# Expert weights of an encoder block: loads of two neighbouring channels per partition, in six places of 22,528 bytes

## Chip, core and metric

The kernel runs on one core of a Trainium2 chip. The metric is the device time of one execution in microseconds (us), as the median of three runs. The core has five engines that run their own instruction streams: TensorE (PE, with PEld for its weight loads), VectorE (DVE), ScalarE (ACT), GpSimd (POOL) and SyncE (SP). SP issues every load here; the bytes are moved by the core's 16 DMA engines.

## What is computed

One layer of an encoder for 512 tokens of 1,024 channels, in float32: a mixing layer (windowed attention beside a gated MLP, then an output projection), and then 16 experts, each of which picks its 64 best tokens. Cut to what matters here:

```python
mod = jax.nn.silu(c) @ w_ada[l] + b_ada[l]
shift1, scale1, gate1, shift2, scale2, gate2 = jnp.split(mod, 6, axis=-1)
h = modulate(rms_norm(x, norm_pre_mix[l]), shift1, scale1)
proj = h @ w_in[l]
...                                              # attention and gated MLP -> mix
x = x + gate1[:, None, :] * rms_norm(mix @ w_out[l], norm_post_mix[l])
h2 = modulate(rms_norm(x, norm_pre_ffn[l]), shift2, scale2)
aff = softmax(h2 @ w_router); gates, idx = top_k(aff^T, 64)          # per expert
xs = h2[idx]
hid = silu(xs @ w_gate[e]) * (xs @ w_up[e])      # w_gate, w_up: 16 x 1024 x 2816
out = (hid @ w_down[e]) * gates                  # w_down: 16 x 2816 x 1024
x = x + gate2[:, None, :] * rms_norm(scatter_add(out, idx), norm_post_ffn[l])
```

The weights of the experts are 16 x 3 x 11.53 MB = 553.6 MB of the 593.6 MB that the kernel reads. Each is used once.

## The kernel before

**Stages.** The kernel is one straight program without loops on the chip. First comes the mixing layer (x transposed, modulations from `w_ada`, input projection, attention, gated MLP, output projection), then the experts, one after the other. Within the mixing layer the steps of attention and projection are interleaved by a hand-written table (`at_step`); a scheduler of the framework then fixes each engine's order, and an engine runs its instructions strictly in that order.

**The weights' loads.** The helper `chunk` (lines 831 to 836) allocates a tile, has SP load it, and returns it. A load of before is 128 partitions of 2,816 float32: 11,264 contiguous bytes for each partition, 1.44 MB in all. `up_proj` takes one load for each of the eight row tiles of 128 channels of `w_gate` or `w_up` (partition p holds channel p of the tile); `expert` takes eight loads for `w_down`. So an expert has 24 loads, and the 16 experts have 384 such pieces.

**Places.** The 13 places of these loads come from four pools, in the order `ORDER`: six in `sl`, whose places serve all loads of the mixing layer too (weights of the input projection, `w_ada`, `w_out`) and which stays open from the first line to the last; three in `s2p`, which hold parts of `w_out` for the gated MLP's half of the output projection (`wz`) until then; three in `s3p` on the right side, over what attention had (`at`, closed behind the last attention step); one in `s4p`, over what the output projection had (`ow`). For the first expert two more loads go to three tiles of the mixing layer (`in_places`). A new tile waits for those that had its bytes before.

**Lanes.** Each DMA takes the next of eight completion semaphores (named DMAHW0 to DMAHW7), and waits for the DMA that had it before. So at most eight are under way.

**An expert.** `route` ranks the tokens and gathers the chosen rows with matmuls (`px`), transposes them and applies scale and shift (`pxt`); `hidden` does the gate and the up projection, multiplies, and transposes the result (`pht`); `expert` does the down projection (`pd`) and adds the rows back with matmuls (`pys`). `last_expert` takes the down projection in three parts of the channels with smaller loads (two DMAs each, runs of 2,048 or 1,024 bytes), so that what follows the last bytes is short.

Of the kernel before, what the change touches and what calls it, by code (L numbers as in the profile page):

```python
# [7 lines left out]
F32 = mybir.dt.float32  # L8
# [21 lines left out]
N1, N2, N3, N4 = 6, 3, 3, 1  # L30
# [5 lines left out]
ORDER = (0,) * N1 + (1,) * N2 + (2,) * N3 + (3,) * N4  # L36
XK = len(ORDER) - KD
# [14 lines left out]
def encoder_block(ctx, tc, x, c, w_ada, b_ada, norm_pre_mix, norm_post_mix, w_in, sink, sgu_ln_g,  # L52
# [33 lines left out]
    prm = ea.tile([P, 2, P], F32, name="prm")  # L86
    col, prows = {}, {}
# [15 lines left out]
    # columns of w_ada for shift1, scale1 of 128 channels with the rows of w_in for q, k, v of these channels  # L103
# [18 lines left out]
    def more_loads():  # L122
        nonlocal wsT, lng, lnb, wst, nsink, wr
        n1 = params(1, (("npf", by_row(norm_pre_ffn[0]), 8), ("pom", by_row(norm_post_mix[0]), 8),
# [9 lines left out]
        nc.sync.dma_start(wr, w_router[0].rearrange("(k p) e -> p k e", p=P))  # L134
# [9 lines left out]
    # ---------------------------------------------------------------- constants  # L144
# [24 lines left out]
    def make_dist():  # L169
        """|distance|, or a huge number outside the window; keys in front of, of, behind the block"""  # L170
# [10 lines left out]
    def rsqrt(dst, v, n):  # L181
        """dst = 1/sqrt(v) for [P, n] f32, to f32's accuracy: a guess from the bits, then Newton."""
# [19 lines left out]
    def rms(src, n, junk, dst=None):  # L202
        """1/rms of the rows of src (one [P, n] or two halves of it)"""
# [12 lines left out]
    # ---------------------------------------------------------------- parameters by column  # L216
    pc = [cp.tile([P, 64], F32, name=f"pc{i}") for i in range(2)]
# [16 lines left out]
    for o in (8, 32):  # L234
        nc.vector.tensor_scalar(pcol("ba", o, 8), pcol("ba", o, 8), 1.0, None, op0=OP.add)

    # ---------------------------------------------------------------- x: transposed; 1 / rms
# [29 lines left out]
    # ---------------------------------------------------------------- shift1, scale1; h  # L267
# [7 lines left out]
    def mod_rows(pm, col, w, n, first, last):  # L275
        """w [P, 4, n]: four column tiles of the array add col^T w at once"""
        for j in range(4):
            nc.tensor.matmul(pm[32 * j:32 * j + 32, :n], col.to_broadcast([P, 32]), w[:, j],
                             start=first, stop=last, tile_position=(0, 32 * j))

    def mod_cols(rows, n):
        """the four rows of rows [P, n] as columns: [P, n / 128, 4] in PSUM"""
# [5 lines left out]
    def mod1_rows(k):  # L288
        """PE: even and odd rows of w_ada in column tiles of their own"""
# [19 lines left out]
    def mod1_acc(k):  # L309
        """DVE: the sums over a partition's rows"""  # L310
# [25 lines left out]
    # ---------------------------------------------------------------- input projection  # L336
# [3 lines left out]
    def split(hi, lo, src):  # L340
        """src as a sum of two parts that float32r holds"""
# [10 lines left out]
    def qkv(k):  # L352
        """heads j and j + 4 of q share a block of rows; then k, v"""
# [43 lines left out]
    param_cols(1, prows[1])  # L397
    nc.vector.tensor_scalar(nsink, nsink, -1.0, None, op0=OP.mult)
# [43 lines left out]
    def attn_out(n, j):  # L442
        """the same heads' outputs, transposed"""
# [32 lines left out]
    def attn_end(n, j0, j1):  # L476
        """heads j0 .. j1 and those 4 on, in two parts, and their squares"""
# [17 lines left out]
    # ---------------------------------------------------------------- gMLP  # L495
# [13 lines left out]
    def spatial():  # L509
        """u (W_s vn + b_s), in place of u"""  # L510
# [25 lines left out]
    # ---------------------------------------------------------------- the other modulations  # L536
# [7 lines left out]
    def mod2(i, kk):  # L544
        """gate1, shift2, scale2, gate2: two row tiles of their columns at a time, summed over a partition's rows"""
# [11 lines left out]
    def mod2_cols(i):  # L557
        pm = bank("pm2")
        mod_rows(pm, ones, acc[i].rearrange("p (j w) -> p j w", j=4), 256, True, True)
# [3 lines left out]
        nc.vector.tensor_tensor(mods[:, i].rearrange("p (j q) -> p q j", j=4), m,  # L563
# [4 lines left out]
        elif i == 2:  # L568
            nc.vector.tensor_tensor(s2, s2, pcol("npf", 0, 8), op=OP.mult)
# [9 lines left out]
    def spread(dst, cols):  # L579
        """dst [P, D]: every row the vector whose columns are given"""  # L580
# [8 lines left out]
    # ---------------------------------------------------------------- the mixing layer, interleaved  # L589
# [495 lines left out]
```

## Time and profile before

| | before |
|---|---|
| median of 3 runs | 1546.35 us (1544.28 to 1550.43) |
| span of the profiled execution | 1544.5 us |
| PE busy / DVE / ACT / POOL | 1387.1 / 429.7 / 188.9 / 116.0 us |
| moved by DMA | 596.86 MB, 386 GB/s over the span |
| loads of 1.44 MB | 128 gate, 126 up, 120 down (and two up loads in parts, 18 + 6 smaller down loads) |

The profiled execution's span, 1544.5 us from its first to its last instruction, lies within the times of the three runs and 1.85 us under their median. It has two regimes. Up to about 270 us the mixing layer runs, with the engines busy and the DMA engines partly idle. From there to about 1,522 us the experts' weights stream in without a pause that a slice of the profile would show. Then a tail of some 22 us finishes the last expert and writes the output. [...]

### The profile page before, as it was taken

To read this page: it belongs to the slowest core of one execution; us is meant where nothing else is said; L and a number is where in the kernel's file an instruction comes from. 1 tells how busy PE (TensorE), PEld (TensorE's weight loads), DVE (VectorE), ACT (ScalarE), POOL (GpSimd) and SP (SyncE) were. 2 spreads that over 40 slices of the span, in tenths; PEclk is the share of its full clock that TensorE was granted. 3 is DMA by queue.
4 is the path that set the end of the run, shared out by engine and by line. 5 is a ranking of instruction groups with operands and counts; after the bars stand their busy time and mean duration, and the time that the engine had idled before them with its cause. 6 is when DMAs were issued, how large, how long until landed. Compare 5 with 4: busy or idle time off the path is not lost.

```text
span 1544.5 us, 17570 instructions
## 1 busy us (share of the span) xinstructions
PE 1387.1 (90%) x7282; PEld 619.8 (40%) x7282; DVE 429.7 (28%) x1087; ACT 188.9 (12%) x404; POOL 116.0 (8%) x144
## 2 busy tenths in 40 slices
PE   7888998999999998998898998989898989898986
PEld 5665665343444433333333333324242423333323
DVE  5789857112112120212112111112020303020104
ACT  3336433000010000000100000000000000000001
POOL 2457310000000000000000000000000000000002
PEclk9998999999999999999999999999999999999998
DMA  9776608999999999999999999999999999999995
GB/s 316 275 252 181 241 6 334 415 411 428 429 429 429 429 429 428 429 428 429 429 428 429 429 429 429 429 428 429 429 428 429 429 429 429 428 429 429 429 396 202
DMA packets 92711, 596.86 MB, mean 386 GB/s; under 512 B 8692, under 2 KB 31960, under 8 KB 44760
## 3 DMA queue, kind: packets, MB, share of 16 engines
q1 hardware_dynamic: 92632, 595.74, 93.3%
q8 instruction: 57, 0.93, 0.2%
q14 instruction: 22, 0.18, 0.0%
HBM read 593.62 MB, written 2.10 MB: 386 GB/s over the span
## 4 chain that ended last, share of the span: by engine, by line
DMA 60%; PE 28%; DVE 8%; issue 1%; ACT 1%; POOL 1%; SPq 0%; DVEq 0%; ACTq 0%; POOLq 0%
DMA w<-in_w_down_dram 23%; DMA w<-in_w_up_dram 19%; DMA w<-in_w_gate_dram 18%; PE pf L949 11%; PE pd L991 4%; PE px L888 1%; PE pys L1001 1%; PE py L348 1%; PE py L346 1%; PE po L462 1%; PE py L347 1%; DVE ex L851 1%; PE pd L1031 1%; DVE racc L555 1%; DVE acc L317 1%
## 5 line engine op out<-in xcount | busy, mean ns | idle before, releaser
L949 PE MATMUL pf<-w,ex 128*64 128x512 f32 (+1 forms) x3072 | 638.0, 561 | 42.0 <-DMA w<-in_w_up_dram 40.6
L949 PEld LDWEIGHTS pf<-w,ex 128*64 128x64 f32 x3072 | 215.0, 137 | 433.2 <-issue 326.2
L991 PE MATMUL pd<-w,ex 128*64 128x512 f32 (+1 forms) x1440 | 319.3, 563 | 33.7 <-DMA w<-in_w_down_dram 33.7
L991 PEld LDWEIGHTS pd<-w,ex 128*64 128x64 f32 x1440 | 109.9, 136 | 231.7 <-issue 126.0
L967 DVE TENSOR_TENSOR ex<-pf,ex 128x512 f32<-128x512 f32 (+1 forms) x48 | 30.4, 647 | 362.3 <-PE pf L949 362.0
L995 DVE TENSOR_SCALAR ex<-pd,gc 128x512 f32<-128x512 f32 x15 | 11.3, 751 | 377.6 <-PE pd L991 377.6
L907 POOL COPY ex<-ex 128x512 f32<-128x512 f32 x16 | 9.8, 613 | 1138.2 <-DVE ex L905 1058.0
L888 PE MATMUL px<-x_sb,ex 128*64 128x256 f32 x512 | 71.0, 386 | 8.6 <-DVE ex L864 7.4
L919 ACT ACTIVATE ex<-pot 128x512 f32<-128x512 f32 x16 | 9.6, 597 | 544.6 <-PE pot L917 544.6
L1007 DVE TENSOR_TENSOR y<-pys,y 128x512 f32<-128x512 f32 x112 | 68.2, 681 | 17.0 <-PE pys L1001 17.0
L974 ACT ACTIVATE ex<-pht 128x512 f32<-128x512 f32 (+1 forms) x48 | 23.5, 559 | 374.6 <-PE pht L973 374.6
L1001 PE MATMUL pys<-ex 64*128 64x512 f32 x240 | 55.6, 602 | 12.7 <-DVE ex L995 12.7
L900 DVE TENSOR_SCALAR ex<-pxt,mods 128x64 f32<-128x64 f32 x128 | 34.9, 337 | 92.0 <-PE pxt L895 92.0
L888 PEld LDWEIGHTS px<-x_sb,ex 128*64 128x64 f32 x512 | 41.3, 136 | 38.3 <-DVE ex L864 18.8
L851 DVE SCALAR_TENSOR_TENSOR ex<-rt,afs,before 128x512 f32<-128x512 f32 (+2 forms) x65 | 46.8, 719 | 12.3 <-PE rt L858 12.3
L913 DVE COPY gc<-pgc 128x1 f32<-128x1 f32 x16 | 2.5, 158 | 152.6 <-PE pgc L910 152.6
L555 DVE SCALAR_TENSOR_TENSOR racc<-ada,cs,racc 128x1024 f32<-128x1024 f32 x28 | 42.6, 1521 | 0.2
L959 ACT ACTIVATE ex<-pf 128x512 f32<-128x512 f32 (+1 forms) x48 | 26.9, 561 | 121.2 <-PE pf L949 120.4
L1001 PEld LDWEIGHTS pys<-ex 64*128 64x128 f32 x240 | 21.9, 186 | 47.1 <-DVE ex L995 25.9
L973 PE MATMUL pht<-ident,ex 128*128 128x128 f32 x176 | 25.7, 295 | 12.1 <-DVE ex L967 12.1
L973 PEld LDWEIGHTS pht<-ident,ex 128*128 128x128 f32 x176 | 22.7, 213 | 22.7 <-DVE ex L967 22.7
L890 ACT ACTIVATE ex<-px 128x256 f32<-128x256 f32 x32 | 12.3, 383 | 125.7 <-PE px L888 125.6
(254 smaller groups left out, 1086.3 us busy)
## 6 DMA issues: line engine op xcount, KB each, us to landing
w<-in_w_gate_dram SPq DMA_DIRECT2D x128, 1408.0 KB, 26.8
w<-in_w_up_dram SPq DMA_DIRECT2D x126, 1408.0 KB, 26.8
w<-in_w_down_dram SPq DMA_DIRECT2D x120, 1408.0 KB, 26.8
ada<-in_w_ada_dram SPq DMA_DIRECT2D x16, 1024.0 KB, 6.5
w<-in_w_down_dram SPq DMA_DIRECT2D x18, 512.0 KB, 9.6
wq<-in_w_ada_dram SPq DMA_DIRECT2D x16, 512.0 KB, 5.9
wi<-in_w_in_dram SPq DMA_DIRECT2D x4, 1024.0 KB, 5.2
wq<-in_w_in_dram SPq DMA_DIRECT2D x8, 384.0 KB, 6.2
```

Source lines behind the costliest of these rows:

```text
L555: nc.vector.scalar_tensor_tensor(acc[i], t[:, r], cs[:, k:k + 1], acc[i], op0=OP.mult, op1=OP.add)
L851: nc.vector.scalar_tensor_tensor(junk[:, :c1 - c0], p[:, c0:c1], afs[:, b, e:e + 1], before[:, o + c0:o + c1], op0=OP.subtract, op1=OP.is_ ...
L888: nc.tensor.matmul(px[i][h * CAP:(h + 1) * CAP, :256], ohr[:, b], x_sb[:, b, c0:c0 + 256], start=(b == 0), stop=(b == NB - 1))
L900: nc.vector.tensor_scalar(xs[:, k], pt[:, c0:c0 + CAP], s2[:, k:k + 1], sh2[:, k:k + 1], op0=OP.mult, op1=OP.add)
L949: nc.tensor.matmul(pb[n][h * 64:(h + 1) * 64, :NW[n]], XS[e][:, k], t, start=(i == 0), stop=(i == KD - 1))
L959: nc.scalar.activation(hid[:, n * 512:n * 512 + NW[n]], pg[n][:, :NW[n]], AF.Silu)
L967: nc.vector.tensor_tensor(hs, pu[n][:, :NW[n]], hs, op=OP.mult)
L973: nc.tensor.transpose(p[:, j * P:(j + 1) * P], hv[:, j0 + j], ident)
L974: nc.scalar.activation(hT[:, j0:j0 + n], p.rearrange("p (j t) -> p j t", j=4)[:, :n], AF.Copy)
L991: nc.tensor.matmul(pd[dh * 64:(dh + 1) * 64, c0:c0 + n], hT[:, j, h * CAP:(h + 1) * CAP], t[:, o - q * FF:o - q * FF + n], start=(h == 0 a ...
L1001: nc.tensor.matmul(p, OT[e][dh * 64:(dh + 1) * 64, b * P:(b + 1) * P], oe[dh * 64:(dh + 1) * 64, :], start=True, stop=True)
L1007: nc.vector.tensor_tensor(yb, p, yb, op=OP.add)
```

## The change

A load now takes two neighbouring channels per partition: partition p of a load of `w_gate` or `w_up` holds channels 2p and 2p + 1 of 256 channels, 22,528 contiguous bytes, 2.88 MB in all; for `w_down` a load is twice as wide as before. An expert has 12 loads. The four pools become two: `wl` with five places on the left side, `wrt` with one on the right. So that they can lie there, `sl` and `s2p` become phases that are closed behind the mixing layer, with `outw`. The first expert's third load of `w_up` goes to the three tiles of the mixing layer, in three DMAs.

Since a partition now has neighbouring channels, all that meets these weights by channel is laid out in pairs: the rows of `w_router`, shift2, scale2 and norm_pre_ffn (`pair_cols`, `prm2`, `pp`), the transposes for the router and for the chosen rows (a step of two in the free axis), and two modulations' columns. The matmuls of an expert's gate and up projections are the same in number and size; those of the down projection are 44 of 512 columns in place of 40 of 512 and 8 of 256.

```diff
-N1, N2, N3, N4 = 6, 3, 3, 1
+N1, N2 = 6, 3
+NL, NR = 5, 1
...
-ORDER = (0,) * N1 + (1,) * N2 + (2,) * N3 + (3,) * N4
-XK = len(ORDER) - KD
+ORDER = (0,) * 3 + (1,) * NR + (0,) * (NL - 3)
+XK = 2 * (len(ORDER) - KD // 2)
...
-    sl = ctx.enter_context(tc.tile_pool(name="sl", bufs=N1))
...
+    closeS, sl = phase("sl", "left", N1)
     closeE, ea = phase("early", "left")
...
+        nc.sync.dma_start(wr.rearrange("p (m i) e -> p m (i e)", i=2),
+                          w_router[0].rearrange("(m p i) e -> p m (i e)", p=P, i=2))
+        nc.sync.dma_start(prm2[:8], b_ada[0, 3 * D:5 * D].rearrange("(r w) -> r w", w=2 * P))
+        nc.sync.dma_start(prm2[8:], norm_pre_ffn[0].rearrange("(r w) -> r w", w=2 * P))
...
+    def pair_cols():
+        p = bank("pp")
+        for i in range(2):
+            nc.tensor.transpose(p[:, i * 12:(i + 1) * 12], prm2[:, i::2], ident[:12, :12])
+        nc.vector.tensor_copy(pp, p[:, :24].rearrange("p (i r) -> p i r", i=2))
+        nc.vector.tensor_scalar(pp[:, :, 4:8], pp[:, :, 4:8], 1.0, None, op0=OP.add)
...
-                nc.tensor.transpose(p[:, k * P:(k + 1) * P], xb[:, (i * 4 + k) * P:(i * 4 + k + 1) * P], ident)
+                c0 = (2 * i + k // 2) * 2 * P
+                nc.tensor.transpose(p[:, k * P:(k + 1) * P], xb[:, c0 + k % 2:c0 + 2 * P:2], ident)
...
-        s2p = ctx.enter_context(tc.tile_pool(name="s2p", bufs=N2, side="left", reuse_waits="tile"))
+        closeW, s2p = phase("s2p", "left", N2)
         closeO, ow = phase("outw", "left")
...
-    closeO.close()
-    s4p = ctx.enter_context(tc.tile_pool(name="s4p", bufs=N4, side="left", reuse_waits="tile"))
-    s3p = ctx.enter_context(tc.tile_pool(name="s3p", bufs=N3, side="right", reuse_waits="tile"))
+    for c in (closeO, closeW, closeS):
+        c.close()
+    wl = ctx.enter_context(tc.tile_pool(name="wl", bufs=NL, side="left", reuse_waits="tile"))
+    wrt = ctx.enter_context(tc.tile_pool(name="wrt", bufs=NR, side="right", reuse_waits="tile"))
...
-    def chunk(ap, shape=(FF,)):
+    def chunk(ap, shape=(2 * FF,)):
...
-        t = (sl, s2p, s3p, s4p)[ORDER[i]].tile([P] + list(shape), F32, name="w", tag="slot")
+        t = (wl, wrt)[ORDER[i]].tile([P] + list(shape), F32, name="w", tag="slot")
...
-        for i, k in enumerate(KORD):
-            rows = [w[0, e, kk * P:(kk + 1) * P, :] for kk in KORD[i:i + 2]]
...
+        for j, m in enumerate(MORD):
+            rows = w[0, e, m * 2 * P:(m + 1) * 2 * P, :].rearrange("(p i) f -> p (i f)", i=2)
+            parts = in_places(rows) if j == extra else [(chunk(rows), 0, 2 * FF)]
+            for i in range(2):
...
-            for q in range(4):
-                t = chunk(wd[:, q * FF:(q + 1) * FF])
...
+            for q in range(2):
+                t = chunk(wd[:, 2 * q * FF:2 * (q + 1) * FF])
```

The order of SP's instructions changes. Before, behind the last two loads of `w_ada` for the mixing layer (`ada`), stand the first loads of `w_gate`, up to those that wait for TensorE; names in brackets are the semaphores that a row waits for: DMAHW0 to DMAHW7 the lanes of earlier DMAs, the others the engines.

```order
L547 DMA ada_1781<-in_w_ada_dram 128x2x1024 [waits DMAHW3_49,DVE_49,Activation_49]
L547 DMA ada_1785<-in_w_ada_dram 128x2x1024 [waits DMAHW4_49,DVE_49,Activation_49]
L835 DMA w<-in_w_gate_dram 128x2816 [waits DMAHW6_49,DMAHW5_49,DVE_49]
L835 DMA w<-in_w_gate_dram 128x2816 [waits DMAHW0_49,DMAHW7_49,DVE_49,Activation_49]
L835 DMA w<-in_w_gate_dram 128x2816 [waits DMAHW1_49,DVE_49]
L835 DMA w<-in_w_gate_dram 128x2816 [waits DMAHW2_49,DVE_49]
L835 DMA w<-in_w_gate_dram 128x2816 [waits DMAHW3_49,DVE_49]
L835 DMA w<-in_w_gate_dram 128x2816 [waits DMAHW4_49,DVE_49]
L835 DMA w<-in_w_gate_dram 128x2816 [waits PE_49] x2
L835 DMA w<-in_w_up_dram 128x2816 [waits DMAHW5_49,PE_49]
L835 DMA w<-in_w_up_dram 128x2816 [waits DVE_49,DMAHW6_49,PE_49,Activation_49]
L835 DMA w<-in_w_up_dram 128x2816 [waits DMAHW7_49,Pool_49]
```

Of the changed kernel, the same place on SP:

```order
L564 DMA ada_1788<-in_w_ada_dram 128x2x1024 [waits DMAHW4_49,DVE_49,Activation_49]
L564 DMA ada_1792<-in_w_ada_dram 128x2x1024 [waits DMAHW5_49,DVE_49,Activation_49]
L857 DMA w<-in_w_gate_dram 128x5632 [waits DVE_49,PE_49,DMAHW6_49,Activation_49,Pool_49]
L953 DMA w<-in_w_up_dram 128x1920 [waits DMAHW7_49,PE_49]
L953 DMA w<-in_w_up_dram 128x1920 [waits DMAHW0_49]
L953 DMA w<-in_w_up_dram 128x1792 [waits DMAHW1_49]
L857 DMA w<-in_w_gate_dram 128x5632 [waits DMAHW4_49,DMAHW3_49,DMAHW2_49]
L857 DMA w<-in_w_gate_dram 128x5632 [waits DVE_49,PE_49,Activation_49]
L857 DMA w<-in_w_gate_dram 128x5632
L857 DMA w<-in_w_up_dram 128x5632 [waits DMAHW5_49]
L857 DMA w<-in_w_up_dram 128x5632 [waits DMAHW6_49]
L857 DMA w<-in_w_up_dram 128x5632 [waits DMAHW7_49,DMAHW2_49,PE_49]
```

What moved: the first load of weights is now that of the place on the right (the fourth of the gate projection), and waits for all five engines' counters; the three parts of the first expert's `in_places` come next; the loads for the places on the left stand behind these. Before, six loads into `sl` stood ahead of the first that waits for TensorE. In the built program the counts behind these names are those of definite instructions. The first load of weights waits for the last matmuls of attention (line 479, which is line 462 before); the first of the three parts waits for the last matmul of the output projection with the attention half's weights (line 364, before 348); the load behind the three parts waits for the lanes of three `ada` loads alone; the next waits for the router's matmuls of the last token block (line 749, before 728) and VectorE's first ranks.

## Rows read from the trace of the kernel before

**Rows 1.** The page's 40 slices: DMA busy in tenths, GB/s moved.
```profile
DMA  9776608999999999999999999999999999999995
GB/s 316 275 252 181 241 6 334 415 411 428 429 429 429 429 429 428 429 428 429 429 428 429 429 429 429 429 428 429 429 428 429 429 429 429 428 429 429 429 396 202
```

**Rows 2.** The page's chain that ended last, shares of the span by engine.
```profile
DMA 60%; PE 28%; DVE 8%; issue 1%; ACT 1%; POOL 1%; SPq 0%; DVEq 0%; ACTq 0%; POOLq 0%
```

**Rows 3.** SP's waits, 620 to 1470 us: waited for, total us, times, longest.
```profile
SPq L835 <- DMA w<-in_w_gate_dram: 263.2, 88, 4.4
SPq L835 <- PE pf L949: 3.1, 13, 0.4
```

**Rows 4.** SP's timeline, groups of eight loads: start, us, line, transfer, count.
```profile
606.26 23.89 SPq L835 DMA_DIRECT2D w<-in_w_gate_dram  x8
...
1471.46 20.07 SPq L835 DMA_DIRECT2D w<-in_w_down_dram  x5
```

**Rows 5.** SP's timeline, single loads of the first expert.
```profile
154.09 0.34 SPq L835 DMA_DIRECT2D w<-in_w_gate_dram  x1
...
180.66 0.33 SPq L835 DMA_DIRECT2D w<-in_w_gate_dram  x1
...
229.85 0.33 SPq L835 DMA_DIRECT2D w<-in_w_gate_dram  x1
...
239.88 0.33 SPq L835 DMA_DIRECT2D w<-in_w_up_dram  x1
...
257.16 0.33 SPq L835 DMA_DIRECT2D w<-in_w_up_dram  x1
257.54 0.94 SPq L931 DMA_DIRECT2D w<-in_w_up_dram  x1
```

**Rows 6.** Stretches: length, busy PE, PEld, DVE, ACT, POOL, PEclk, DMA share, GB/s.
```profile
192.00:229.00 37.00, 35.07 (x211) 25.21 (x210) 19.58 (x79) 14.19 (x38) 4.95 (x11) 0.91 0.00 1
230.00:235.00 5.00, 4.94 (x32) 3.40 (x30) 2.60 (x11) 3.06 (x10) 0.36 (x1) 1.00 0.87 303
251.50:258.00 6.50, 3.59 (x27) 2.60 (x27) 5.49 (x22) 1.93 (x5) 0.00 (x0) 0.74 0.18 74
269.00:272.00 3.00, 3.00 (x18) 1.10 (x16) 0.00 (x0) 0.00 (x0) 0.00 (x0) 1.00 0.68 219
310.00:340.00 30.00, 28.42 (x145) 12.82 (x143) 6.21 (x10) 1.47 (x3) 0.00 (x0) 1.00 0.99 407
510.00:1470.00 960.00, 867.13 (x4358) 330.82 (x4356) 164.20 (x387) 52.34 (x104) 6.74 (x11) 1.00 1.01 429
```

**Rows 7.** PE's timeline, end of the mixing layer: start, us, line, operation, count.
```profile
238.57 1.24 PE L462 MATMUL po<-pT,v_sb 128*64 128x128 f32 x14
...
247.14 0.39 PE L348 MATMUL py<-wo,mix 128*128 128x512 f32 x1
...
255.33 1.09 PE L728 MATMUL pl<-hT,wsp 128*32 128x128 f32 x16
```

**Rows 8.** The chain in order of time: gate, up, down of the first expert.
```profile
266.61 19.05 PE pf L949 x96
...
293.96 18.42 PE pf L949 x92
...
315.35 19.10 PE pd L991 x88
```

**Rows 9.** DMA packets of 67 to 78, 1508 to 1520 and 600 to 1400 us.
```profile
DMA packets 1497, 4.53 MB, mean 412 GB/s; under 512 B 64, under 2 KB 64, under 8 KB 1494
...
DMA packets 4180, 4.18 MB, mean 348 GB/s; under 512 B 137, under 2 KB 4154, under 8 KB 4179
...
DMA packets 34228, 342.90 MB, mean 429 GB/s; under 512 B 3798, under 2 KB 3798, under 8 KB 3798
```

**Rows 10.** PE's timeline in the last expert.
```profile
1494.95 2.58 PE L949 MATMUL pf<-w,ex 128*64 128x512 f32 x12 [0.79 <-DMA w<-in_w_up_dram]
...
1499.80 11.40 PE L1031 MATMUL pd<-w,ex 128*64 128x512 f32 x46
...
1513.40 1.94 PE L1031 MATMUL pd<-w,ex 128*64 128x256 f32 x14
```

**Rows 11.** The line of the router's transposes: duration ns min/median/max, first and last start.
```profile
L712 PE MATMUL ph<-ident,x_sb x32: 271/273/438, 189.5 to 254.3; 128*128 128x128 f32 x32
```

More of the change, by code (lines that the diff above doesn't have):

```diff
@@ L86, in encoder_block @@
     prm = ea.tile([P, 2, P], F32, name="prm")
+    prm2 = ea.tile([12, 2 * P], F32, name="prm2")
     col, prows = {}, {}
@@ L214, in rms @@
         return r
-    pc = [cp.tile([P, 64], F32, name=f"pc{i}") for i in range(2)]
+    pc = [cp.tile([P, n], F32, name=f"pc{i}") for i, n in enumerate((64, 32))]
     def pcol(nm, k, n=1):
@@ L233, in encoder_block @@
     nc.vector.tensor_tensor(cs, cs, pcol("c", 0, 8), op=OP.mult)
-    for o in (8, 32):
-        nc.vector.tensor_scalar(pcol("ba", o, 8), pcol("ba", o, 8), 1.0, None, op0=OP.add)
+    nc.vector.tensor_scalar(pcol("ba", 8, 8), pcol("ba", 8, 8), 1.0, None, op0=OP.add)
+    pp = cp.tile([P, 2, 12], F32, name="pp2")
+    def pair_cols():
[4 more added lines that the diff above has]
+        nc.vector.tensor_scalar(pp[:, :, 4:8], pp[:, :, 4:8], 1.0, None, op0=OP.add)
     junk = ea.tile([P, D], BF16, name="junk")
@@ L277, in mod_rows @@
         for j in range(4):
-            nc.tensor.matmul(pm[32 * j:32 * j + 32, :n], col.to_broadcast([P, 32]), w[:, j],
-                             start=first, stop=last, tile_position=(0, 32 * j))
+            o = pm[32 * j:32 * j + 32, :n]
+            if len(w.shape) == 4:
+                o = o.rearrange("p (q w) -> p q w", q=w.shape[2])
+            nc.tensor.matmul(o, col.to_broadcast([P, 32]), w[:, j], start=first, stop=last, tile_position=(0, 32 * j))
     def mod_cols(rows, n):
@@ L397, in encoder_block @@
     param_cols(1, prows[1])
+    pair_cols()
     nc.vector.tensor_scalar(nsink, nsink, -1.0, None, op0=OP.mult)
@@ L558, in mod2_cols @@
         pm = bank("pm2")
-        mod_rows(pm, ones, acc[i].rearrange("p (j w) -> p j w", j=4), 256, True, True)
+        pairs = i in (1, 2)
+        mod_rows(pm, ones, acc[i].rearrange("p (j w q) -> p j q w", j=4, q=2) if pairs else
+                 acc[i].rearrange("p (j w) -> p j w", j=4), 256, True, True)
         rows = at.tile([P, 256], F32, name="rows2", tag="pT", bufs=4)
@@ L922, in encoder_block, with up_proj @@
     NW = [512, 512, FH - 1024]
-    CUT = FH + 512
-    KORD = (0, 4, 1, 5, 2, 6, 3, 7)
+    CUTS = (0, FH + 512, 2 * FH + 1024, 2 * FF)
+    MORD = (0, 2, 1, 3)
     def in_places(ap):
-        a, b, c = place(0, [2048], F32, "w"), place(1, [2, FF - CUT], F32, "w"), place(5, [2048], F32, "w")
-        for i, t in enumerate((a, c)):
-            nc.sync.dma_start(t[:, :CUT], ap[i][:, :CUT])
-            nc.sync.dma_start(b[:, i], ap[i][:, CUT:])
-        return [(a, b[:, 0]), (c, b[:, 1])]
-    def up_proj(e, w, extra=KD):
-        pb = [bank("pf") for _ in range(3)]
-        ts = {}
-        for i, k in enumerate(KORD):
-            rows = [w[0, e, kk * P:(kk + 1) * P, :] for kk in KORD[i:i + 2]]
-            if i == extra:
-                ts[k], ts[KORD[i + 1]] = in_places(rows)
-            elif k not in ts:
-                t = chunk(rows[0])
-                ts[k] = t, t[:, CUT:]
-            for n in range(3):
-                for h in range(2):
-                    o = h * FH + n * 512
-                    t = ts[k][0][:, o:o + NW[n]] if o < CUT else ts[k][1][:, o - CUT:o - CUT + NW[n]]
-                    nc.tensor.matmul(pb[n][h * 64:(h + 1) * 64, :NW[n]], XS[e][:, k], t,
-                                     start=(i == 0), stop=(i == KD - 1))
+        out = []
+        for i, (c0, c1) in zip((0, 1, 5), zip(CUTS, CUTS[1:])):
+            t = place(i, [2048], F32, "w")
+            nc.sync.dma_start(t[:, :c1 - c0], ap[:, c0:c1])
+            out.append((t, c0, c1))
+        return out
+    def up_proj(e, w, extra=None):
+        pb = [bank("pf") for _ in range(3)]
+        for j, m in enumerate(MORD):
+            rows = w[0, e, m * 2 * P:(m + 1) * 2 * P, :].rearrange("(p i) f -> p (i f)", i=2)
+            parts = in_places(rows) if j == extra else [(chunk(rows), 0, 2 * FF)]
+            for i in range(2):
+                for n in range(3):
+                    for h in range(2):
+                        o = i * FF + h * FH + n * 512
+                        t, c0 = next((t, c0) for t, c0, c1 in parts if c0 <= o < c1)
+                        nc.tensor.matmul(pb[n][h * 64:(h + 1) * 64, :NW[n]], XS[e][:, 2 * m + i],
+                                         t[:, o - c0:o - c0 + NW[n]], start=(j == 0 and i == 0),
+                                         stop=(j == 3 and i == 1))
         return pb
@@ L983, in expert @@
             wd = w_down[0, e, h * FH:(h + 1) * FH, :].rearrange("(p j) d -> p (j d)", j=NJ)
[L984 to L994 removed]
+            for q in range(2):
+                t = chunk(wd[:, 2 * q * FF:2 * (q + 1) * FF])
+                for o in range(0, 2 * FF, 512):
+                    j, dh = divmod((2 * q * FF + o) // 512, 2)
+                    nc.tensor.matmul(pd[dh * 64:(dh + 1) * 64, :], hT[:, j, h * CAP:(h + 1) * CAP], t[:, o:o + 512],
+                                     start=(h == 0 and j == 0), stop=(h == 1 and j == NJ - 1))
         nc.vector.tensor_scalar(oe, pd, GC[e], None, op0=OP.mult)
```

26 lines of the change are left out of this document (8 added, 18 removed).

## Prediction

> **What bounds the kernel now.** I read the 40 slices first [rows 1]. The reader is to see three things there: one slice at 6 GB/s (193 to 232 us), a ramp, and from then on 428 or 429 GB/s in nearly every slice, to the end. So the experts run at the pace of the DMA engines, and what counts is when their stream starts and how fast it runs. The chain confirms it: 60% of the span is DMA [rows 2]. Then SP's waits in the steady stretch: a load is held back by an earlier load in its lane (263.2 us for the gate loads alone, 88 times), hardly ever by a place that TensorE has not freed (3.1 us) [rows 3]. In 510 to 1470 us the DMA share is 1.01 at 429 GB/s [rows 6]. Places are not short there.
>
> The pace comes from SP's groups of eight loads. At 606.26 us the first gate load of expert 5 is issued, at 1471.46 us the first down load of expert 15 [rows 4]. Between them lie 32 groups, 256 loads: 865.2 / 256 = 3.380 us per load of 1.44 MB. Since a load waits for the one eight places before it, 369 loads have landed at 1471.46 us (load 376 is issued, counted from 0, and 368 has landed). What follows takes 1544.5 - 1471.5 = 73.0 us. That is my anchor: when have 369 loads' worth of bytes landed in the changed kernel?
>
> **The start of the stream.** Before, six gate loads are issued between 154.09 and 180.66 us, into places of the mixing layer that VectorE has done with [rows 5]; then SP waits for `wz`, and from 192 to 229 us 1 GB/s moves [rows 6]. The loads go on at 229.85 us [rows 5]. In the changed order no weight load stands ahead of the one on the right, and that waits for the last attention matmuls. This is how a place that is free at 180 us is not loaded at 180 us: the load behind the three parts needs nothing but `ada` loads that have long landed, yet SP is in order, and it stands behind two waits on TensorE. The last attention group starts at 238.57 and lasts 1.24 us [rows 7]; before, the load that waits for it is issued at 239.88 us [rows 5], and so will be the first load now. Behind it wait all loads of the first expert; TensorE waits for its first gate weights in turn.
>
> From issue to flow: before, the restart at 229.85 us gives 303 of 429 GB/s in 230 to 235 us [rows 6], 3.5 us of flow, so it flows from about 231.4, 1.5 us after issue. Now: flow from 241.4. The first 2.88 MB take 6.8 us, to 248.2. The three parts wait for the last output projection matmul, 247.14 + 0.39 us [rows 7]; with 1.5 us to flow they start at 249.0, a gap of 0.8 us. The next load needs nothing more, the one after it the router's matmuls (255.33 + 1.09 us) and VectorE's first ranks; its counterpart before is issued at 257.16 [rows 5, 7], while the third load's bytes flow until 262.5. So the stream has no other gap: it behaves as if it started at 242.2 us.
>
> **Do the six places hold it up?** The eighth load of 2.88 MB is the first that needs a place to be used up (gate's first). Its turn comes at 242.2 + 7 x 6.76 = 289.5 us. Gate's first weights are third in the queue and land near 263; TensorE begins its gate matmuls at 266.61 and needs 19.05 / 4 = 4.8 us for each 2.88 MB [rows 8], so the place is free at 271.4, 18 us early. One expert later: the seventeenth load, expert 1's first of the up projection, has its turn at 242.2 + 16 x 6.76 = 350.4 and needs a place read by the down matmuls that begin at 315.35 and end 19.1 us later [rows 8]. Free 15 us early. The pauses of before (74 GB/s in 251.5 to 258, 219 in 269 to 272, 407 in 310 to 340 [rows 6]) go; they are in the anchor.
>
> At the old pace, then, the 369 loads' bytes have landed at 242.2 + 369 x 3.380 = 242.2 + 1247.2 = 1489.4 us, 17.9 us later than before. In other words: six loads no longer hidden cost 6 x 3.38 = 20.3 us, the restart 10.0 us later costs these, and some 12 us of pauses that disappear come back.
>
> **The pace.** Packets double from 11,264 to 22,528 bytes. No row has a packet of that size from a load, so I bound it. At 429 GB/s a packet of 11,264 bytes takes one of 16 engines 16 x 11264 / 429 = 420 ns. Shorter packets [rows 9]: 1508 to 1520 us has 348 GB/s with runs of 1,024 bytes, 47.1 ns each; 67 to 78 us has 412 GB/s with 3,168 bytes on average (4.53 MB in 1,430 packets), 123 ns. Lines through these and the long packet cut at 9.8 and 6.7 ns: a fixed part per packet, half of which goes for each 11,264 bytes. That is 1.2% or 0.8% of the pace. The other end is 0: the share is 1.01 already, and the limit may be bytes alone. I take 0.6%, between 0 and the nearer row's 0.8% and closer to that, since the short stretches also carry mixed sizes: 0.006 x 1247 = 7.5 us less; the range keeps 0 to 15 us. Fewer loads save nothing by themselves: issues are 3.4 us apart and take 0.33 us each, eight deep [rows 4, 5].
>
> [...]
>
> **The rest.** The down projection's 44 matmuls of 512 columns have the columns of before; nothing on the path. In front of the restart the change adds two small transposes, a copy and an addition (`pair_cols`), and transposes that read with a step of two: the plain ones take 273 ns [rows 11], eight per token block, three blocks before 239.88 us. If the step costs nothing: 0; if it doubled what a transpose adds to the queue, some 1 us a block: 3. I take 1 us; TensorE is busy 35.07 of 37 us there [rows 6]. A gain has no cause.
>
> The tail: TensorE finishes the last up load 2.58 us after it begins, and starts the down matmuls at 1499.80 [rows 10]. With 2.88 MB to work off it starts 2.4 us later. Its first down part takes 11.40 us for 46 matmuls, where the later part runs 14 of half the width in 1.94 us; at 0.217 us (19.10 / 88 [rows 8]) 46 need 10.0, so 1.4 us are waits for weights that absorb part of it. Cost 1.0 us, between 0 and 2.4. Each row tile still has its own matmuls, and the last loads are unchanged.
>
> **Sum.** 242.2 + 1247.2 - 7.5 + 73.0 + 1.0 + 1.0 = 1556.9 us of span, 12.4 above 1544.5. The median lies 1.85 us over the span: 1558.8, rounded to 1559.
>
> **Rivals.** (a) No gain of pace: bytes bound the engines. For it: 429 in every slice whatever the matrix. Against: both rows of short packets. 1559 + 7.5 = 1566.5. (b) The other side: the longer packet pays more than the late start costs. Place: the steady stretch; price: 12.5 us for each 1%. At 1.0% (-12.5) the time is 1554, where it begins to be no change that a measurement can tell (0.5% of 1546, 7.7 us, is about that limit); from 1.6%, 20 us, it is not slower at all, about 1546. For it: the line through the shortest packets gives 1.2%, 1551. Against: 1.6% would need 436 GB/s, and no slice or stretch that I read holds more than 429 [rows 1, 6]. (c) Six places hold the loads back: a place comes free only when 24 matmuls have read all of it. If each expert lost what the stretch 310 to 340 us lost (22 GB/s of 429 over 30 us, 1.5 us), 15 experts would add 23: 1582. Against: the 15 to 18 us in hand above. (d) The change does not do what its order says, and free places are loaded at 154 to 181 us as before: 20.3 us less, 1538.5. Against: SP's order leaves it no way.
>
> **Chances.** Forecast 0.55 (1555 to 1563); (a) 0.22; (b) 0.14 for 1549 to 1554 and 0.02 for less; (c) 0.05; (d) 0.02. Slower by over 0.5%: 0.55 + 0.22 + 0.05 = 0.82. Within 0.5%: 0.14 + 0.01. Faster: 0.03. The range takes in (a) with its 3 us of strided transposes and most of (b): 1550 to 1569.
>
> **What would show it.** Right: no weight load on SP between the last `ada` issue and about 240 us; two or three slices of the 40 near 0 GB/s in place of one; from about 249 us no slice under 425; the last expert's down matmuls from about 1499.8 + 17.9 - 7.5 + 1.0 + 2.4 = 1513.6 us; packets some 24,000 fewer; a pace per 2.88 MB of 6.72 us against 6.76. Wrong: loads of weights at 154 us (d); waits of SP for TensorE in the steady stretch (c); a pace of 6.76 or more (a), or under 6.69 (b).

## The result, and the profile after

The changed kernel takes 1566.07 us (median of 4 runs, 1564.92 to 1567.03), the kernel before in the same comparison 1547.34 us: a ratio of 1.0119, 95% interval 1.0102 to 1.0136. It is slower by 18.7 us, as forecast in sign, and 7 us beyond the predicted 1559, inside the range. The profiled execution's span is 1564.5 us against 1544.5.

The 40 slices of the kernel after (DMA busy in tenths, GB/s) and its packets answer to [rows 1]:

```profile
DMA  9876008999999999999999999999999999999995
GB/s 294 283 251 185 13 1 357 430 428 428 430 428 429 430 427 430 429 428 430 429 427 430 430 428 429 428 428 429 429 428 430 428 430 427 430 427 429 429 379 203
DMA packets 65131, 596.81 MB, mean 381 GB/s; under 512 B 5176, under 2 KB 28448, under 8 KB 41120
```

Two slices stand near zero in place of one (13 and 1 GB/s; before, 241 and 6). The ramp is steeper (357, then 430 at once; before 334, 415, 411). The plateau is the same 427 to 430. There are 27,580 packets fewer than the 92,711 of before: the 24,000 of the weights' loads that were predicted, and 3,516 under 512 bytes that were not counted. Most of these, 3,004, are packets of 4 bytes, of which each load has one on each of the 16 DMA engines (before, from 600 to 1400 us, 3,798 beside the packets of about 237 loads of 1.44 MB [rows 9], 16.0 for each): with half the loads, half of them go. The other 512 belong to parameters now loaded in longer rows.

SP's timeline of the kernel after (start, duration, line, transfer, count) answers to [rows 5]; L857 issues the loads, L953 the three parts:

```profile
149.83 3.75 SPq L564 DMA_DIRECT2D ada<-in_w_ada_dram  x2
238.12 0.34 SPq L857 DMA_DIRECT2D w<-in_w_gate_dram  x1
245.82 1.29 SPq L953 DMA_DIRECT2D w<-in_w_up_dram  x3
247.22 8.94 SPq L857 DMA_DIRECT2D w<-in_w_gate_dram  x3
256.21 15.72 SPq L857 DMA_DIRECT2D w<-in_w_up_dram  x3
```

And TensorE's timeline there (start, duration, line, operation, count), the counterparts of [rows 7]:

```profile
236.73 1.24 PE L479 MATMUL po<-pT,v_sb 128*64 128x128 f32 x14
...
245.39 0.40 PE L364 MATMUL py<-wo,mix 128*128 128x512 f32 x1
...
253.60 1.10 PE L749 MATMUL pl<-hT,wsp 128*32 128x128 f32 x16
```

No weights are asked for between 150 and 238 us. The first load goes out when the last attention group ends (236.73 + 1.24 = 237.97), the parts when the last output projection matmul ends (245.79). The waits are the ones that the order showed.

Stretches of the kernel after (length, busy PE, PEld, DVE, ACT, POOL, PEclk, DMA share, GB/s), against [rows 6]; the last one, 150 to 400 us, is new and sums up the start:

```profile
192.00:229.00 37.00, 35.07 (x226) 25.39 (x226) 21.43 (x86) 14.91 (x40) 4.95 (x11) 1.00 0.00 1
...
251.50:258.00 6.50, 4.94 (x35) 3.91 (x34) 4.38 (x22) 1.85 (x7) 0.00 (x0) 0.50 1.01 418
...
269.00:272.00 3.00, 3.00 (x19) 1.23 (x15) 0.00 (x0) 0.00 (x0) 0.00 (x0) 1.00 0.99 428
...
310.00:340.00 30.00, 28.41 (x137) 10.46 (x135) 6.38 (x11) 1.47 (x3) 0.00 (x0) 1.00 1.00 429
510.00:1470.00 960.00, 855.99 (x4240) 331.44 (x4236) 165.17 (x399) 53.60 (x107) 7.36 (x12) 1.00 1.00 429
...
150.00:400.00 250.00, 229.85 (x1302) 126.61 (x1303) 109.77 (x366) 58.49 (x149) 23.08 (x35) 0.97 0.67 281
```

The same stretch of the kernel before:

```profile
150.00:400.00 250.00, 232.83 (x1323) 128.44 (x1325) 108.12 (x366) 57.05 (x144) 21.06 (x34) 0.97 0.77 313
```

The pauses of before are gone (418, 428 and 429 GB/s where it had 74, 219 and 407). Yet over 250 us the kernel after moves (313 - 281) x 250 = 8.0 MB less, and at 429 GB/s those take 18.6 us (rounding leaves 0.6 us either way). That is nearly all of the 20.0 us by which the spans differ. From 510 to 1470 us both move 429 GB/s.

SP's waits from 620 to 1470 us (waited for, total us, times, longest) look quite different from [rows 3]:

```profile
SPq L857 <- PE pf L968: 431.4, 72, 9.0
SPq L857 <- PE pd L1008: 244.7, 44, 7.1
SPq L857 <- PE pot L938: 60.9, 10, 6.1
SPq L857 <- DMA w<-in_w_down_dram: 42.8, 43, 2.3
```

So does the chain that ended last, against [rows 2]:

```profile
PE 55%; DMA 33%; DVE 7%; issue 1%; ACT 1%; SPq 1%; POOL 1%; DVEq 0%; ACTq 0%; POOLq 0%
```

Read alone, these two say that TensorE has become the bound and that places are short. The stretch above says that they are not: the DMA share is 1.00 throughout. With six places, SP waits for a place to come free, where with thirteen it waited for a lane; but at that moment several loads are still queued (35.2 us from issue to landing at the median of the gate loads by the page, five times the 6.7 us that 2.88 MB take at 429 GB/s), and the DMA share stays at 1.00. A chain follows the last release, and the last release was TensorE's; the rate did not depend on it, as the experiment with moved places shows below.

### The profile page after: what moved, and what is told of

It reads as the page before. It is cut to its first block, busy times and chain, and to the rows that moved or that the text cites. A ratio compares the mean times of both kernels' runs of the same rounds, so it can differ in the third digit from the quotient of the medians.

```text
span 1564.5 us, 16946 instructions
## 1 busy us (share of the span) xinstructions
PE 1384.7 (89%) x7164; PEld 618.8 (40%) x7164; DVE 429.7 (27%) x1088; ACT 188.6 (12%) x404; POOL 115.0 (7%) x144
## 4 chain that ended last, share of the span: by engine, by line
PE 55%; DMA 33%; DVE 7%; issue 1%; ACT 1%; SPq 1%; POOL 1%; DVEq 0%; ACTq 0%; POOLq 0%
DMA w<-in_w_down_dram 30%; PE pf L968 29%; PE pd L1008 6%; PE px L910 4%; PE pys L1016 4%; DMA w<-in_w_up_dram 2%; PE pd L1046 1%; PE pgc L931 1%; PE po L479 1%; PE py L364 1%; PE py L362 1%; PE py L363 1%; DVE racc L572 1%; DVE ex L873 1%; DVE ex L1010 1%
## 5 line engine op out<-in xcount | busy, mean ns | idle before, releaser
L968 PE MATMUL pf<-w,ex 128*64 128x512 f32 (+1 forms) x3072 | 630.4, 560 | 35.1 <-DMA w<-in_w_up_dram 33.9
L968 PEld LDWEIGHTS pf<-w,ex 128*64 128x64 f32 x3072 | 223.1, 137 | 417.0 <-issue 335.3
L1008 PE MATMUL pd<-w,ex 128*64 128x512 f32 x1320 | 320.6, 599 | 51.1 <-DMA w<-in_w_down_dram 51.1
L1008 PEld LDWEIGHTS pd<-w,ex 128*64 128x64 f32 x1320 | 98.3, 137 | 262.0 <-issue 172.6
L359 POOL TENSOR_TENSOR wl<-wi,wh 128x512 fp32r<-128x512 f32 x16 | 23.9, 1498 | 22.0 <-ACT wh L358 22.0
## 6 DMA issues: line engine op xcount, KB each, us to landing
w<-in_w_gate_dram SPq DMA_DIRECT2D x64, 2816.0 KB, 35.2
```

The source lines that it names most:

```text
L968: nc.tensor.matmul(pb[n][h * 64:(h + 1) * 64, :NW[n]], XS[e][:, 2 * m + i], t[:, o - c0:o - c0 + NW[n]], start=(j == 0 and i == 0), stop=( ...
L1008: nc.tensor.matmul(pd[dh * 64:(dh + 1) * 64, :], hT[:, j, h * CAP:(h + 1) * CAP], t[:, o:o + 512], start=(h == 0 and j == 0), stop=(h == 1 ...
```

## Experiments

Times are medians. "Per expert" is the distance from expert 5's first gate issue on SP to expert 15's, divided by ten (81.00 us before, 81.14 after). About every 220 to 240 us (64 to 72 loads of 1.44 MB, or half as many of 2.88) the stream falls some 1.0 to 1.6 us back, in most kernels here at one group, in the ones of experiments six and seven over several; what that is stays open. In the kernel before a packet of 16,384 bytes from an instruction queue (57 of them in the span) starts within each of the four late gaps (of some 4.7 us) from 620 to 1470 us; such a packet comes about every 28 us, most without a late load, so this is a lead and not a cause. A "quiet" expert is the distance between two such issues without it.

**One: the late start alone.** The kernel before keeps its small loads and thirteen places, but `sl` and `s2p` are closed behind the mixing layer, and ten places lie in one pool behind them, three in one on the right.

```diff
-ORDER = (0,) * N1 + (1,) * N2 + (2,) * N3 + (3,) * N4
+ORDER = (0,) * 6 + (1,) * 3 + (0,) * 4
-    sl = ctx.enter_context(tc.tile_pool(name="sl", bufs=N1))
+    closeS, sl = phase("sl", "left", N1)
-        s2p = ctx.enter_context(tc.tile_pool(name="s2p", bufs=N2, side="left", reuse_waits="tile"))
+        closeW, s2p = phase("s2p", "left", N2)
-    closeO.close()
-    s4p = ctx.enter_context(tc.tile_pool(name="s4p", bufs=N4, side="left", reuse_waits="tile"))
-    s3p = ctx.enter_context(tc.tile_pool(name="s3p", bufs=N3, side="right", reuse_waits="tile"))
+    for c in (closeO, closeW, closeS):
+        c.close()
+    wl = ctx.enter_context(tc.tile_pool(name="wl", bufs=10, side="left", reuse_waits="tile"))
+    wrt = ctx.enter_context(tc.tile_pool(name="wrt", bufs=3, side="right", reuse_waits="tile"))
```

> The kernel before with loads of 1.44 MB, 13 places and its own layout of channels, but its pools closed behind the mixing layer and opened anew as in the changed kernel (ten places left, three right). No weight load then stands ahead of the waits for attention. Theory (late start): the stream starts near 240 us in place of 154, everything else as before: 1547.3 + 18 = 1565 us (1562 to 1568), the first 1.44 MB of weights after 235 us. Rival (size of places and loads): 1547, as before.

Measured: 1566.34 us, ratio 1.0117 (1.0102 to 1.0133). Its slices and its stretch from 150 to 400 us:

```profile
GB/s 324 259 254 187 4 1 341 428 429 428 429 428 428 428 429 429 430 429 428 428 429 428 428 429 429 429 428 427 429 428 429 428 430 429 428 429 428 429 399 205
```

```profile
150.00:400.00 250.00, 233.89 (x1317) 135.94 (x1319) 109.21 (x366) 57.72 (x146) 21.96 (x34) 0.95 0.66 278
```

(313 - 278) x 250 / 429 = 20.4 us' worth of bytes are missing at 400 us, and the time is 19.1 us longer than that of the kernel before in the same comparison (1547.21). Without one longer packet or larger place, the closing of the pools alone loses as much as the whole change.

**Two: the changed kernel with an early start.** Its left pool is split, so that three places lie over what the mixing layer frees first and are not held back by the rest.

```diff
-ORDER = (0,) * 3 + (1,) * NR + (0,) * (NL - 3)
+ORDER = (0,) * 3 + (1,) * NR + (2,) * (NL - 3)
-    wl = ctx.enter_context(tc.tile_pool(name="wl", bufs=NL, side="left", reuse_waits="tile"))
+    wl = ctx.enter_context(tc.tile_pool(name="wl", bufs=3, side="left", reuse_waits="tile"))
+    wm = ctx.enter_context(tc.tile_pool(name="wm", bufs=NL - 3, side="left", reuse_waits="tile"))
```

> The changed kernel with its left pool cut in two: three places over the mixing layer's old load places, two behind them. Loads, sizes and the six places are those of the changed kernel; only the first three loads of the gate weights stand on SP ahead of the waits for attention. Theory (the start of the stream is what the change lost): three loads of 2.88 MB are issued between 155 and 185 us again, 20.3 us are hidden again; the eighth load still waits for the first 2.88 MB to be used up (about 271 us), so one load of 1.44 MB and some 2 us stay lost, and 1 us in the tail: 1552 us (1549 to 1555). Rival (the double-size places hold the stream back all along): the time stays at 1566.

Measured: 1557.34 us, ratio 1.0067 (1.0052 to 1.0082), 81.0 us per expert. SP's timeline and two stretches:

```profile
174.91 65.77 SPq L858 DMA_DIRECT2D w<-in_w_gate_dram  x4
```

```profile
150.00:400.00 250.00, 232.86 (x1295) 126.43 (x1297) 108.11 (x366) 57.05 (x144) 21.03 (x34) 0.95 0.72 298
...
272.00:299.00 27.00, 25.54 (x148) 11.03 (x146) 6.61 (x22) 3.05 (x6) 0.61 (x1) 1.00 0.89 371
```

The second stretch in the changed kernel:

```profile
272.00:299.00 27.00, 25.54 (x149) 12.05 (x151) 6.61 (x22) 4.33 (x7) 0.61 (x1) 1.00 1.00 427
```

Three loads, 8.6 MB, go out early again (four issues from 174.91 on, the last of them at 240.4 us), and 8.7 of the 18.7 us come back; the expectation of 1552 was missed by 5. Against before, (313 - 298) x 250 / 429 = 8.7 us are still missing at 400 us. Part of that is the restart at 240.4 in place of 229.85 us [rows 5]: the fourth load stands on the right, behind attention. The other part is new: 371 GB/s at a DMA share of 0.89 in 272 to 299 us, where the changed kernel has 427 at 1.00. The author's explanation is that the stream, started early, catches up with TensorE, and that a place of 2.88 MB then comes free late; SP's waits in this stretch are not shown.

**Three: are bytes the only limit?** Each place of the changed kernel is loaded by two DMAs, one channel each: the same places, packets of 11,264 bytes as before.

```diff
-        for o, i in zip([t[:, h] for h in range(len(ap))], ap) if isinstance(ap, list) else [(t, ap)]:
+        for o, i in zip([t[:, h] for h in range(len(ap))], ap) if isinstance(ap, list) else [(t[:, :FF], ap[:, :FF]), (t[:, FF:], ap[:, FF:])]:
```

> The changed kernel, each place filled by two DMAs of 11,264 bytes per partition in place of one of 22,528: the packet length is undone alone. Theory (the engines are bound by bytes, a packet's length is worth nothing between 11 and 22 KB): 1566 us, within 2, and 81.1 us for an expert in the steady stretch. Rival (the long packets do gain 5 to 10 us, and something else eats it): 1571 to 1576.

Measured: 1584.08 us, ratio 1.0237 (1.022 to 1.0254). The theory of the expectation falls, and the time lies beyond its rival's 1571 to 1576 too. Its steady stretch, SP's waits, and two gate groups of SP's timeline (eight DMAs now for four places):

```profile
510.00:1470.00 960.00, 862.64 (x4215) 328.75 (x4210) 165.06 (x399) 54.19 (x108) 7.36 (x12) 1.00 1.01 423
```

```profile
SPq L857 <- DMA w<-in_w_down_dram: 257.5, 85, 3.1
...
SPq L857 <- PE pf L968: 0.7, 3, 0.4
```

```profile
1043.82 24.04 SPq L857 DMA_DIRECT2D w<-in_w_gate_dram  x8
...
1125.34 24.07 SPq L857 DMA_DIRECT2D w<-in_w_gate_dram  x8
```

With the packet size of before it runs at 423 GB/s, where before runs at 429; a quiet expert takes 81.52 us, and SP waits for lanes again, not for places. Two things follow. Longer packets in fewer loads do gain: 429 against 423 in the same places (packets and loads are both doubled in number here; the last section says what share is the loads'). And something else in the changed kernel costs about as much.

**Four: packets count, from the other end.** The kernel before with two DMAs for each load, of alternate quarters: runs of 2,816 bytes.

```diff
-            nc.sync.dma_start(o, i)
+            if isinstance(ap, list):
+                nc.sync.dma_start(o, i)
+            else:
+                for q in range(2):
+                    nc.sync.dma_start(*(v.rearrange("p (r q f) -> p q r f", q=2, r=2)[:, q] for v in (o, i)))
```

> The kernel before, each load of 1.44 MB as two DMAs that take alternate quarters of a partition's row: runs of 2,816 bytes, four packets in place of one, twice as many DMAs. It prices a packet where it can be seen four times. Theory (bytes bind, a packet costs nothing that lasts): 1547 us, within 4. [...] The lines of the prediction through the short packets (6.7 to 9.8 ns): 1607 to 1634.

Measured: 1600.27 us, ratio 1.0341 (1.0318 to 1.0364).

```profile
510.00:1470.00 960.00, 853.78 (x4171) 322.00 (x4172) 160.62 (x385) 52.86 (x106) 6.75 (x11) 1.00 1.04 411
```

It runs at 411 GB/s and 84.5 us per expert, so four times the packets cost 3.5 us per expert; the time lies 53 us above the theory's 1547 and 7 under the 1607 to 1634 that the prediction's lines gave. This is not clean: with twice the DMAs the eight lanes cover half the bytes, and SP waits some 107 us for TensorE's gate, up and down matmuls between 620 and 1470 us:

```profile
SPq L839 <- PE pf L953: 56.7, 61, 2.3
SPq L839 <- PE pd L995: 50.2, 72, 2.0
```

It bounds the price of a packet from above: 3.5 us over 576 more packets for each DMA engine is 6.1 ns. The shortest rows' 9.8 ns and the next rows' 6.7 of the prediction [rows 9] lie above it.

**Five: where the places start.** What differs between experiment three and the kernel before is where in a partition the places lie. In the built programs ten of the thirteen places of before start at a multiple of 256 bytes, and three, on the right, 224 bytes past one. In the changed kernel all six start 224 bytes past one: its own small tiles (64 columns become 32 in one, 96 bytes are added in another) push everything on the left down by 32 bytes. So: the changed kernel with idle columns ahead of both pools, which put all six places on multiples of 256.

```diff
+    cp.tile([P, 8], F32, name="pad")
...
+    pr_ = ctx.enter_context(tc.tile_pool(name="padr", bufs=1, side="right"))
+    pr_.tile([P, 56], F32, name="padr")
```

> The changed kernel with its six places moved to addresses that are multiples of 256 bytes in a partition (32 bytes of padding on the left, 224 on the right); nothing else. In the changed kernel all six start 224 bytes behind a multiple of 256, in the kernel before ten of 13 start at one. Theory (a packet pays a fixed part and, at an odd start, a second one; the split run's 27.18 us for eight loads, before's 26.80 and the changed kernel's 53.7 give 2.8 and 7.7 ns): the quiet pace per 2.88 MB falls from 6.71 to 6.65 us, 11 us over the stream: 1555 us (1552 to 1559). Rival (where a place starts is of no account, the split loads were slow because of their number or their pitch): 1566.

Measured: 1558.78 us, ratio 1.0091 (1.0074 to 1.0107): 7.3 us less than the changed kernel, by 256 bytes of padding per partition (6.5 us, if each is taken against the kernel before in its own comparison). Its steady stretch, and two gate groups of SP's timeline:

```profile
510.00:1470.00 960.00, 862.03 (x4279) 334.71 (x4277) 166.16 (x399) 53.64 (x107) 7.36 (x12) 1.00 1.00 432
```

```profile
617.78 20.70 SPq L860 DMA_DIRECT2D w<-in_w_gate_dram  x4
...
697.81 20.70 SPq L860 DMA_DIRECT2D w<-in_w_gate_dram  x4
```

432 GB/s; a quiet expert takes 80.03 us. Of the changed kernel:

```profile
1188.48 20.86 SPq L857 DMA_DIRECT2D w<-in_w_gate_dram  x4
...
1269.01 20.86 SPq L857 DMA_DIRECT2D w<-in_w_gate_dram  x4
```

80.53 us. TensorE's work is the same in both, and the rate rose: the chain's 55% of PE was not the bound.

**Six and seven: the same in the kernel before.** With 32 bytes of padding on the left, its ten left places leave the multiples of 256 (the three on the right stay 224 past one); with 224 bytes on the right instead, all thirteen stand on a multiple.

```diff
+    cp.tile([P, 8], F32, name="pad")
```

> The kernel before with 32 bytes of padding in front of its ten left places, so that none of the 13 starts at a multiple of 256 bytes. Theory (start of the place): eight loads take 27.18 us in place of 26.80, as in the split run: 1547 + 18 = 1565 us (1561 to 1569). Rival (pitch or number of loads made the split run slow): 1547.

```diff
+    pr_ = ctx.enter_context(tc.tile_pool(name="padr", bufs=1, side="right"))
+    pr_.tile([P, 56], F32, name="padr")
```

> The kernel before with 224 bytes of padding on the right, so that the three right places start at multiples of 256 bytes too; the ten left ones do already. Theory: 3 of 13 loads get 7.7 ns of 425 per packet back, 0.4% of the stream: 1542 us (1540 to 1545), faster than both kernels. Rival: 1547.

Measured: 1561.71 us, ratio 1.0109 (1.0087 to 1.0131), and 1546.98 us, ratio 1.0007 (0.9997 to 1.0017). SP's gate groups, shifted first, then all aligned:

```profile
1099.90 24.11 SPq L836 DMA_DIRECT2D w<-in_w_gate_dram  x8
...
1181.58 24.09 SPq L836 DMA_DIRECT2D w<-in_w_gate_dram  x8
```

```profile
1010.12 23.72 SPq L837 DMA_DIRECT2D w<-in_w_gate_dram  x8
...
1090.67 23.73 SPq L837 DMA_DIRECT2D w<-in_w_gate_dram  x8
```

Shifted, a quiet expert takes 81.68 us, aligned 80.55, which is what before takes (the group after the one at 606.26 us [rows 4] begins at 686.81). So a shift of 32 bytes makes the kernel before 1% slower, but bringing its last three places into line gains nothing. The second was not expected. In the kernel before, nearly all packets of these loads have the same time by the trace, 422 ns, those to the three odd places included (98.7% of all, from 600 to 1400 us); shifted, 7% have it, and most take 426 or 433 ns. Why three odd places of thirteen cost nothing where all six, or ten of thirteen, do is open.

**Eight and nine: is it 256 bytes, or only the odd 32?** Both kernels with their left places 64 bytes past a multiple of 256: ten of thirteen in the kernel before (the other three 224 past), and five of six in the changed one. The place on its right stood on a multiple, so that the expectation's "each" holds for five. Shown against the edits of experiments five and six:

```diff
-    cp.tile([P, 8], F32, name="pad")
+    cp.tile([P, 24], F32, name="pad")
```

> The changed kernel with the six places moved so that each starts 64 bytes past a multiple of 256 (before this study's padding 224 past it; in e5_pairs_aligned at a multiple, 80.47 us per expert). Theory A, any start that is no multiple of 256 bytes costs: 81.1 us per expert and 1566 us, as the changed kernel. Theory B, a start that is a multiple of 64 bytes is free and only one that is 32 bytes off costs: 80.5 us per expert and 1558 to 1559 us. Nothing else moves: the late start stays in both.

```diff
+    cp.tile([P, 16], F32, name="pad")
```

> The kernel before with its ten places on the left moved from multiples of 256 bytes to 64 bytes past one (e6_singles_shifted had them 32 bytes past: 82.00 us per expert). Theory A, any start that is no multiple of 256 costs: 82.0 us per expert, some 1559 to 1562 us. Theory B, multiples of 64 are free: 81.0 us per expert, 1547 us.

Measured: 1565.55 us, ratio 1.0112 (1.0094 to 1.0131), and 1561.77 us, ratio 1.009 (1.0064 to 1.0117). Gate groups, the changed kernel's form first:

```profile
621.10 20.83 SPq L860 DMA_DIRECT2D w<-in_w_gate_dram  x4
...
701.42 20.83 SPq L860 DMA_DIRECT2D w<-in_w_gate_dram  x4
```

```profile
610.89 24.07 SPq L836 DMA_DIRECT2D w<-in_w_gate_dram  x8
...
692.28 24.15 SPq L836 DMA_DIRECT2D w<-in_w_gate_dram  x8
```

80.32 and 81.39 us in a quiet expert, 80.9 and 81.8 per expert: theory A, as far as 64 bytes go; a start 128 bytes past a multiple was not tried. A start 64 bytes past a multiple of 256 costs too, if somewhat less: 0.29 us per quiet expert for the pairs, where all six places 224 past cost 0.50; 0.84 for the singles, where 32 past cost 1.13.

The padding moves the other tiles on the left too, so it could be one of these that counts. The changed kernel's form of this run speaks against that. Taken by the trace in the order of their starts, the packets in the turn of the one place on a multiple go down to 836.4 ns on average, those in the turns of the places 64 past are at up to 840.7, in the same execution. All six on multiples (experiment five) take 836 ns.

So starts 32, 64 and 224 bytes past a multiple of 256, where most places stand so, cost 0.29 to 1.13 us per quiet expert against all places on a multiple. A start 32 past costs no less than one 224 past: with packets of 11,264 bytes a quiet expert takes 81.68 us at starts 32 past (ten of 13, experiment six) and 81.52 at starts 224 past (all six places, experiment three), against 80.55 with all on multiples (experiment seven). Why such a start costs, no run shows.

**Ten: both repairs together.** The changed kernel with the early start of experiment two and the padding of five.

> The first experiment (pairs, left pool cut in two, early start) with the six places at multiples of 256 bytes. Theory: its 1557.3 less 11: 1546 us (1543 to 1550), level with the kernel before: start and place together account for the change's loss, and the long packet then gives some 4 us against aligned singles, which the coarser places at the start take away. Rival (place of no account): 1557.

Measured: 1546.57 us, ratio 0.9998 (0.9982 to 1.0014).

```profile
310.00:340.00 30.00, 28.42 (x137) 10.47 (x135) 5.43 (x9) 1.47 (x3) 0.00 (x0) 1.00 0.97 399
510.00:1470.00 960.00, 860.83 (x4272) 332.70 (x4270) 163.07 (x387) 53.43 (x106) 6.75 (x11) 1.00 1.00 432
...
150.00:400.00 250.00, 231.38 (x1310) 124.41 (x1311) 110.77 (x367) 59.49 (x150) 23.75 (x35) 0.97 0.73 303
```

It reaches 432 GB/s, and loses (313 - 303) x 250 / 429 = 5.8 us at the start, to the later restart (238.90 us in place of 229.85 [rows 5]) and, by the author's reading, to the coarse places (399 GB/s from 310 to 340 us). Gain and loss are alike: level with the kernel before, not better.

## Why the prediction was right, and where it was off

The spans differ by 20.0 us, the prediction had 12.4. The time lies inside the stated range but outside the forecast's own 1555 to 1563: the range was wide enough to take in rival (a), and the time came out at (a)'s 1566.5 for a reason that the prediction did not have. In that, the range held by luck.

- **The late start** was predicted at 17.9 us, and 1.0 more for the mixing layer; 18.6 were measured by 400 us. Experiment one, which has this step alone, is 19.1 us slower than before; experiment two, which takes it back in part, wins 8.7. The waits were the ones named. The first load went out at 238.12 us, 1.8 earlier than predicted, so the added transposes and copies cost nothing that can be seen in front of it; the parts went out at 245.82 where 247.5 was implied.
- **The pauses that go**: right. From 251.5 us to 1470 no stretch shown is under 418 GB/s.
- **The six places**: right in what counts, wrong in its sign. The stream never pauses for a place (1.00, 429 GB/s), so rival (c) falls. But the sign named for (c), waits of SP for TensorE in the steady stretch, is there with 431.4 + 244.7 us. It was a bad sign: SP's wait says which release came last, not that the DMA engines had nothing left to do. Only the DMA share can tell that.
- **The pace** is the term that was mis-sized: predicted -7.5 us, measured +0.3. When the last up load has been taken up TensorE's row stands at 1513.89 us against 1494.95 [rows 10], 18.9 later, so after the 18.6 of the start nothing was won or lost up to there. This is the size of rival (a), but not its mechanism. Bytes alone don't bound the engines: in the same places, packets of 22,528 bytes ran at 429 GB/s and packets of 11,264 at 423. The step that failed is the silent one that the packets' size is all that changes about a load; where the places start changed too, and cost what the longer packets gained. (That fewer loads save nothing by themselves was nearly right: the 4-byte packets are, by the estimate of the last section, about a fifth of what is gained.) With the starts on multiples of 256 the gain is there: 80.03 against 80.55 us per quiet expert, 0.65%, where 0.6% was taken. Neither the diff nor the rows show the new starts; the addresses of the built program would have.
- **The tail**: predicted +1.0, measured 20.0 - 18.9 = 1.1. The rows, against [rows 10]:

```profile
1513.89 4.94 PE L968 MATMUL pf<-w,ex 128*64 128x512 f32 x24 [1.78 <-DMA w<-in_w_up_dram]
...
1521.11 10.09 PE L1046 MATMUL pd<-w,ex 128*64 128x512 f32 x46
```

The last up load takes 4.94 us in place of 2.58, the down part 10.09 in place of 11.40: the waits in it absorbed 1.3 us, 1.4 were predicted.

Of the rivals, (d) fell with the timeline (no weights before 238 us), and the other side, (b), with the 429 GB/s. Even without the odd starts, (b) would have won 8 us against 20 lost.

## What to carry to other kernels

When a pool is moved behind others to make room for larger tiles, ask which loads its places took early, and behind which waits the first one stands now; here that (18.6 us by 400 us) outweighed what the longer packet gave on aligned starts (0.52 us per quiet expert, some 8 us in all). When SP waits for a place, look at the DMA share before calling places short. And look at the start addresses of the tiles that a stream fills: here small tiles that grew and shrank elsewhere put all six places 224 bytes past a multiple of 256, at 80.53 us per quiet expert in place of 80.03.

## What the runs showed of the hardware

Per packet and DMA engine, worked out from the quiet experts (an expert is 192 packets of 11,264 bytes or 96 of 22,528 for each of the 16 engines); behind each figure stands its experiment or kernel:

| start past a multiple of 256 bytes | 11,264 bytes | 22,528 bytes | twice the short less the long |
|---|---|---|---|
| 0 | 419.5 ns (seven) | 833.6 ns (five) | 5.4 ns |
| 224 | 424.6 ns (three) | 838.9 ns (changed kernel) | 10.3 ns |
| 64 (ten of 13, five of 6) | 423.9 ns (nine) | 836.7 ns (eight) | |
| 32 (ten of 13) | 425.4 ns (six) | | |

Split into a part that grows with the bytes and a fixed part for each packet (an estimate from these four figures), both rows have the same time for the bytes, 414 ns for 11,264, and the fixed part is 5.4 ns where the packet starts on a multiple of 256 bytes, about twice that where it starts 224 past. Not all of it is the packet's own: every load has a 4-byte packet on each engine, 9 ns by the trace of the kernel before, and with eight packets for each engine and load that is 1.1 ns of the 5.4. By this estimate the fixed part is what a longer packet in a load twice as large halves, and the 6.7 and 9.8 ns that the prediction drew from short packets were both somewhat high for an aligned one. Open are why a start off a multiple costs, the three odd places of the kernel before that cost nothing, a start 128 bytes past a multiple, and the late group about every 230 us.
